# A two-layer decoder trunk on one core: the recurrent stage ordered by hand on four engines

## The chip, the core and the metric

The kernel runs on one core of a Trainium2 chip. A core has TensorE (matrix products, PE in the profile), VectorE (DVE), ScalarE (ACT), GpSimd (POOL), SyncE (SP, which here only issues DMAs), and DMA engines between the chip's memory and its own. The engines run side by side, each takes its own instructions strictly in order, and they wait for each other by semaphores. The metric is the device time of one execution in microseconds (us). Before the change it is 925.75 us, the median of three runs (925.34 to 928.98).

## What is computed

The input x is 1024 tokens by 1024 features, all float32. Two layers run one after the other; each has a projection, a token mixer, an attention over 256 fixed memory tokens, a SiLU gate, an output projection and a layer norm:

```python
for layer in range(2):
    if layer == 0:                      # multi-head latent attention, 12 heads
        z = h @ mla_w_in
        c_q, c_kv, k_r, gate, q_mem = split(z)
        q = rms_norm(c_q) @ w_uq;  kv = rms_norm(c_kv) @ w_ukv      # rotary part added
        tok = causal_attention(q, k, v)
    else:                               # recurrent branch, 768 channels
        z = h @ lru_w_in
        u, gate, q_mem = split(z)
        xc = conv_b + sum over 4 taps of shifted u * conv_w          # causal
        r = sigmoid(blockdiag(xc, w_r) + b_r);  i = sigmoid(blockdiag(xc, w_i) + b_i)
        log_a = (-8 * softplus(-lam)) * r;  a = exp(log_a)
        g = sqrt(-expm1(2 * log_a)) * (i * xc)
        tok[s] = a[s] * tok[s-1] + g[s]                              # scan over the tokens
    mem_out = softmax(q_mem @ mem_k.T / 8) @ mem_v                   # 4 heads, 256 tokens
    y = concat(tok, mem_out) * silu(gate)
    h = layer_norm(alpha * h + y @ w_out)
```

## The kernel before

Every float32 operand of a product is split into a rounded high part and the low rest, and one product is three matmuls: high by high, high by low, low by high (`mm3`, lines 110 to 115). The high part is a copy that rounds, made by ACT or POOL; the low part is a subtraction that only VectorE makes (`split`, lines 88 to 90). A weight tile comes by DMA into one of two stages `wf`, is split into a pair of buffers (a ring of two pairs, `R16`/`R17` and `rg0`/`rg1`), and is then used (`load_w`, line 100): the next load into a stage waits until both parts of the last have been made, and the next split into a pair waits until the products with the last are over.

The order on each engine comes from a scheduler that goes by the order of the code and by its own estimates, and may put later work first, except inside `manual_schedule`, where the engines named there keep the order of the code.

The stages, with their times in the profile: the compressed inputs and gates of layer 0 (to about 200 us), the causal attention (to about 440), the memory attention of layer 0 (to about 500), the output projection and layer norm of layer 0 (to about 593), the recurrent stage (593 to 710), the gate products (two of them to 733, the others between the units of the next stage), the memory attention of layer 1 (to about 807), the output projection of layer 1.

**Attention and the maxima rows.** Work is done in units of 512 columns: TensorE makes scores, ACT takes the exponential twice (full and rounded), and the low part is their difference (line 564), made by POOL, for every fourth unit by VectorE; TensorE then multiplies both parts with the values three units later. Between the units stands filler: the scores of the heads of the next pair, from which VectorE takes the row maxima (`max_pass`, lines 439 to 462). When a head's maxima are known, `neg_max_row` (line 427) puts a small job in a list: TensorE transposes the negated maxima (line 433), VectorE copies them (line 435), SP sends them by DMA into row 96 of that head's queries (line 436). The job is run `DELAY = 3` units later by `flush_rows`. The third score matmul of each tile of that head reads row 96 (97 rows, line 657).

**The products with the reciprocals.** When a pair of heads is done, `finish_pair` (line 624) sends the sums of the exponentials through memory and back as reciprocals, spread over the lanes, and POOL multiplies the pair's tile with them (line 634). The slots are 0 to 5 for the causal heads, 6 and 7 for the memory pairs of layer 0, 8 and 9 for those of layer 1. SP also loads layer norm's vectors into the same buffers `Of` afterwards.

**The recurrent stage** goes over six tiles t of 128 channels by 1024 tokens. `u`(t) is the projection on TensorE: 48 matmuls of 512 columns. `c`(t) copies it out of the PSUM banks (ACT, two halves, line 1015). `v`(t) is the convolution on VectorE (line 1020 and three times line 1023), then the high part XH (ACT, line 84) and the low part XL (VectorE, line 90). `r`(t) is all the rest (`lru_rest`): 12 gate matmuls of XH and XL with WGH and WGL, sigmoid (line 1036), exponential, tanh and square on ACT (lines 1038, 1039, 1041), three products and the scan on VectorE (lines 1040, 1042, 1044, 1045), a square root on ACT between them (line 1043). The code has `c0 v0 c1 v1 r0 u2 c2 v2 r1 u3 ...`, then the two projections of the memory queries (`q0`, `q1`) and two gate products (`g6`, `g7`). The weights of u0 and u1 come early into buffers of the attention; those of u2 to u5 are loaded in `lru_u`, and the gate weights WGH/WGL, both halves, before `c0`.

Of the kernel before, what the change touches and what calls it, by code (L numbers as in the profile page):

```python
# [20 lines left out]
S = 1024  # L21
# [23 lines left out]
def hybrid_kernel(ctx: ExitStack, tc: tile.TileContext, io):  # L45
# [209 lines left out]
    def qmem_proj(layer, m, ap, mh, ml, thi, tlo, ps):  # L255
        hi, lo = load_w(ap, S)
        proj_T(ps, hi, lo, mh, ml, 8)
        for n, cs in enumerate(HALF):
            ACT.copy(thi[n], ps[n])
            DVE.tensor_tensor(out=tlo[n], in0=ps[n], in1=f32(thi[n]), op=ALU.subtract)  # L260
            SP.dma_start(qmem_d[layer][m, 0][:, cs], f32(thi[n]))
            SP.dma_start(qmem_d[layer][m, 1][:, cs], f32(tlo[n]))

    for m in range(2):
        qmem_proj(0, m, io["w0"][8 + m], lambda n: [x[:, HALF[n]] for x in xh], lambda n: [x[:, HALF[n]] for x in xl],
                  ph[2 * m:2 * m + 2], pl[2 * m:2 * m + 2], next_ps())
# [160 lines left out]
    def neg_max_row(mx, dst_row):  # L427
# [9 lines left out]
        rows.append([DELAY, row])  # L437

    def max_pass(h, halves=None):
# [21 lines left out]
        neg_max_row(mx, lambda: sets[h % 4][2][96:97, :])  # L461
# [162 lines left out]
    def finish_pair(gt, slot):  # L624
# [9 lines left out]
        POOL.tensor_tensor(out=gt, in0=gt, in1=rec, op=ALU.mult)  # L634
# [325 lines left out]
    ring["hi"], ring["lo"] = [sets[i][2] for i in (1, 2, 3)], [sets[i][3] for i in (1, 2, 3)]  # L960
    u_ps = []
    for t in range(2):
        hi, lo = load_w(io["w1"][t], S)
        ps = pair(t)
        proj_T(ps, hi, lo, hth, htl, 8)
        u_ps.append(ps)
# [5 lines left out]
    ring["hi"], ring["lo"] = [R16, rg[0]], [R17, rg[1]]  # L972
    pc = open_pool("pc")
# [10 lines left out]
    for i in range(2):  # L984
        j = wjob[0]
        wjob[0] += 1
        SP.dma_start(wf[j % 2][:, 0:768], io["wg"][i])
        split(wf[j % 2][:, 0:768], WGH[:, i * 768:(i + 1) * 768], WGL[:, i * 768:(i + 1) * 768], POOL)

# [27 lines left out]
    def lru_conv(t):  # L1017
# [7 lines left out]
        split(xc, XH[b], XL[b], ACT)  # L1025

    def lru_rest(t):
# [52 lines left out]
    ORD = 'c0 v0 c1 v1 r0 u2 c2 v2 r1 u3 c3 v3 r2 u4 c4 v4 r3 u5 c5 v5 r4 q0 r5 q1 g6 g7'  # L1080
    for it in ORD.split():
        t = int(it[1])
        if it[0] == 'c':
            lru_copy(t, u_ps[t])
        elif it[0] == 'v':
            lru_conv(t)
        elif it[0] == 'r':
            lru_rest(t)
        elif it[0] == 'u':
            lru_u(t)  # L1090
        elif it[0] == 'g':
            gate_load(t)
            run_all(gate1(t, next_p()))
        else:
            qmem_proj(1, t, io["w1"][14 + t], hth, htl, [QH[:, c] for c in HALF], [QL[:, c] for c in HALF], next_p())
# [123 lines left out]
```

## Time and profile before

| | us |
|---|---|
| three runs, median (lowest to highest) | 925.75 (925.34 to 928.98) |
| the profiled execution, its own time | 924.84 |
| its span, first to last instruction | 923.0 |
| TensorE busy in the span | 896.5 (97%) |
| VectorE, ScalarE, GpSimd busy | 592.2 (64%), 443.1 (48%), 222.9 (24%) |
| mean granted TensorE clock, as a share of full speed | 0.992 |

The profile is one execution, 1.8 us longer outside its span than within it. A row of the timeline gives the start, the duration, the engine, the line and the operation with its tiles, and in brackets how long the engine had been idle before it and which instruction released it. Busy time of TensorE includes the overlap of pipelined matmuls, so that consecutive starts, not durations, give its pace. VectorE, ScalarE and GpSimd are far from full over the whole span, and nearly full in the recurrent stage.

### The profile page before, as it was taken

The page shows a single profiled execution, that of the slowest core. Times are in us where ns is not written, and L with a number is a line of the kernel's source. Part 1 is how long each engine was busy: PE and PEld are TensorE (multiplying, and loading weights), DVE is VectorE, ACT ScalarE, POOL GpSimd, SP SyncE. Part 2 cuts the span into 40 slices and gives each one's busy share as a digit, 9 for nine tenths or more (in the row PEclk, how much of TensorE's full clock was granted, in tenths as well). Part 3 has the DMA queues.
Part 4 walks back from the last instruction along what each step waited for, and adds up shares of the span by engine and source line. Part 5 has one row for each costly group of instructions (what it writes and reads, how often), then busy time and mean ns, then how long its engine had stood idle before and what let it go on. Part 6 is the DMA issues. An engine that isn't in the chain of part 4 may idle for free.

```text
span 923.0 us, 12452 instructions
## 1 busy us (share of the span) xinstructions
PE 896.5 (97%) x4477; PEld 735.2 (80%) x4477; DVE 592.2 (64%) x1207; ACT 443.1 (48%) x764; POOL 222.9 (24%) x219
## 2 busy tenths in 40 slices
PE   9999999999999999999999999988999999999996
PEld 8998888877787788778777888867888877678886
DVE  7953346258867767796775497646997154457655
ACT  4422311217676667777795122107997156753000
POOL 5100023101526364563672200000000032210000
PEclk9999999999999999999999999998999999999998
DMA  9103133314022213056657653111113921252411
GB/s 328 45 15 109 55 100 127 128 63 111 23 61 70 59 58 104 13 144 178 194 150 207 197 194 125 50 51 47 45 46 113 220 69 47 69 184 91 155 73 46
DMA packets 45945, 96.08 MB, mean 104 GB/s; under 512 B 10906, under 2 KB 20282, under 8 KB 45884
## 3 DMA queue, kind: packets, MB, share of 16 engines
q1 hardware_dynamic: 45308, 94.47, 32.7%
q8 instruction: 35, 0.57, 0.3%
q10 hardware_dynamic: 576, 0.82, 0.3%
q14 instruction: 26, 0.21, 0.1%
HBM read 71.94 MB, written 23.16 MB: 103 GB/s over the span
## 4 chain that ended last, share of the span: by engine, by line
PE 82%; DVE 7%; ACT 3%; issue 3%; DMA 2%; POOL 2%; SPq 0%; DVEq 0%; ACTq 0%; POOLq 0%
PE bank L113 10%; PE bank L115 10%; PE bank L114 10%; PE bank L858 6%; PE bank L860 6%; PE bank L859 6%; PE bank L572 6%; PE bank L657 5%; PE bank L367 3%; PE bank L369 3%; PE bank L368 3%; PE bank L154 2%; PE bank L155 2%; PE bank L153 2%; PE bank L454 2%
## 5 line engine op out<-in xcount | busy, mean ns | idle before, releaser
L564 POOL TENSOR_TENSOR pl<-Pf,ph 128x512 fp32r<-128x512 f32 (+1 forms) x99 | 124.6, 1268 | 116.4 <-ACT ph L562 93.6
L561 ACT ACTIVATE Pf<-bank 128x512 f32<-128x512 f32 (+1 forms) x152 | 86.3, 568 | 50.3 <-DVE bank L558 20.8
L657 PE MATMUL bank<-st,st 96*128 96x512 f32 (+7 forms) x432 | 105.5, 342 | 0.1
L90 DVE TENSOR_TENSOR R<-wf,R 128x1024 fp32r<-128x1024 f32 (+4 forms) x43 | 48.8, 1138 | 65.6 <-POOL R L82 59.8
L657 PEld LDWEIGHTS bank<-st,st 96*128 96x128 f32 (+1 forms) x432 | 75.7, 189 | 13.0 <-DVE st L403 0.5
L562 ACT ACTIVATE ph<-bank 128x512 fp32r<-128x512 f32 (+1 forms) x136 | 76.2, 561 | 0.2
L82 POOL TENSOR_SCALAR R<-wf 128x1024 fp32r<-128x1024 f32 (+3 forms) x25 | 24.4, 979 | 200.1 <-PE bank L114 97.3
L113 PE MATMUL bank<-R,R 128*128 128x256 f32 (+1 forms) x190 | 63.2, 333 | 0.7 <-ACT Pf L375 0.4
L114 PE MATMUL bank<-R,R 128*128 128x256 f32 (+1 forms) x190 | 62.3, 328 | 0.1
L115 PE MATMUL bank<-R,R 128*128 128x256 f32 (+1 forms) x190 | 62.2, 327 | 0.0
L456 DVE CUSTOM_DVE_ANT_0 bank<-bank,cmask 128x384 f32<-128x384 f32 (+3 forms) x96 | 48.8, 517 | 9.8 <-PE bank L454 9.0
L123 ACT ACTIVATE rq_t<-lnv 128x1 f32<-128x1 f32 x16 | 3.3, 203 | 101.7 <-DVE lnv L909 101.7
L367 PE MATMUL bank<-xh,R 128*128 128x512 f32 x128 | 50.8, 397 | 0.1
L369 PE MATMUL bank<-xh,R 128*128 128x512 f32 x128 | 50.7, 396 | 0.0
L368 PE MATMUL bank<-xl,R 128*128 128x512 f32 x128 | 50.5, 395 | 0.0
L572 PE MATMUL bank<-ph,VH 128*65 128x512 f32 (+2 forms) x144 | 49.2, 342 | 0.0
L572 PE MATMUL bank<-pl,VH 128*65 128x512 f32 (+2 forms) x144 | 44.8, 338 | 2.2 <-POOL pl L564 1.2
L572 PE MATMUL bank<-ph,VL 128*65 128x512 f32 (+2 forms) x144 | 47.0, 337 | 0.0
L859 PE MATMUL bank<-wo,yh 128*128 128x512 f32 (+1 forms) x126 | 46.8, 371 | 0.0
L858 PE MATMUL bank<-wo,yh 128*128 128x512 f32 (+1 forms) x126 | 46.6, 369 | 0.0
L860 PE MATMUL bank<-wo,yl 128*128 128x512 f32 (+1 forms) x126 | 46.0, 369 | 0.0
L904 DVE SCALAR_TENSOR_TENSOR GA<-GA,bank 128x512 f32<-128x512 f32 (+1 forms) x34 | 22.0, 647 | 37.1 <-PE bank L860 37.1
(315 smaller groups left out, 2447.1 us busy)
## 6 DMA issues: line engine op xcount, KB each, us to landing
wf<-w SPq DMA_DIRECT2D x26, 512.0 KB
wf<-wout SPq DMA_DIRECT2D x16, 512.0 KB
Of<-den_d SPq DMA_DIRECT2D x20, 256.0 KB
GA<-x SPq DMA_DIRECT2D x8, 512.0 KB
h_d<-GA SPq DMA_DIRECT2D x8, 512.0 KB
GA<-h_d SPq DMA_DIRECT2D x8, 512.0 KB
y_d<-GA SPq DMA_DIRECT2D x7, 512.0 KB
out<-GA SPq DMA_DIRECT2D x7, 512.0 KB
```

The lines of the kernel that those rows point to most:

```text
L113: PE.matmul(out, lh, rh, start=(i == 0), stop=False)
L114: PE.matmul(out, lh, rl, start=False, stop=False)
L115: PE.matmul(out, ll, rh, start=False, stop=(i == n - 1))
L367: PE.matmul(ps[n], hi[:, ks], xh[k][:, cs], start=(k == 0), stop=False)
L369: PE.matmul(ps[n], lo[:, ks], xh[k][:, cs], start=False, stop=(k == 7))
L561: ACT.activation(pf[:, :n], ps[:, :n], AF.Exp, scale=scale)
L564: lo_eng.tensor_tensor(out=lo[:, :n], in0=pf[:, :n], in1=f32(hi)[:, :n], op=ALU.subtract)
L572: mm.append(lambda: PE.matmul(ops[0:65, q0:q0 + w], st, mv[:, c0:c0 + w], start=start, stop=stop))
L657: yield lambda: PE.matmul(ps[:, c0:c0 + w], k[0:r, ks], q[0:r, qs], start=(i == 0), stop=(i == 2))
L858: PE.matmul(out, hi, woh[k][:, ns], start=(k == ko[0]), stop=False)
L859: PE.matmul(out, hi, wol[k][:, ns], start=False, stop=False)
L860: PE.matmul(out, lo, woh[k][:, ns], start=False, stop=(k == ko[7]))
```

## The change

1. The recurrent stage is cut into finer pieces, and their order is written out for VectorE, ScalarE, GpSimd and TensorE at once (`manual_schedule`): `x` is the low part XL, `s` the gate matmuls and sigmoids, `i` the product of input gate and convolution, `e` exponential, tanh and square, `n` the product under the root, `z` root, product and scan, `w` the second half of the gate weights, `l`, `k`, `h` loads and splits of weights ahead of their use.
2. XH is copied by GpSimd, not ScalarE.
3. The weights of u2 and u3 are loaded and split before u0's products, the first half of the gate weights after them, the second half between tiles 0 and 1. u1's weights go into another free pair of attention buffers.
4. The products with the reciprocals of slots 7, 8 and 9 are made by VectorE, not GpSimd.
5. The maxima row of an even head is run 5 units after its maxima, not 3.

```diff
-    def neg_max_row(mx, dst_row):
+    def neg_max_row(mx, dst_row, delay=DELAY):
...
-        rows.append([DELAY, row])
+        rows.append([delay, row])
...
-        neg_max_row(mx, lambda: sets[h % 4][2][96:97, :])
+        neg_max_row(mx, lambda: sets[h % 4][2][96:97, :], 5 if h % 2 == 0 else DELAY)
...
-        POOL.tensor_tensor(out=gt, in0=gt, in1=rec, op=ALU.mult)
+        eng = DVE if slot >= 7 else POOL
+        eng.tensor_tensor(out=gt, in0=gt, in1=rec, op=ALU.mult)
...
-    ring["hi"], ring["lo"] = [sets[i][2] for i in (1, 2, 3)], [sets[i][3] for i in (1, 2, 3)]
+    ring["hi"], ring["lo"] = [sets[i][2] for i in (1, 3)], [sets[i][3] for i in (1, 3)]
     u_ps = []
+    uw = [load_w(io["w1"][t], S) for t in range(2)]
+    ring["hi"], ring["lo"] = [R16], [R17]
+    gw = {2: load_w(io["w1"][2], S)}
     for t in range(2):
-        hi, lo = load_w(io["w1"][t], S)
+        hi, lo = uw[t]
...
     ring["hi"], ring["lo"] = [R16, rg[0]], [R17, rg[1]]
+    gw[3] = load_w(io["w1"][3], S)
...
-    for i in range(2):
+
+    def lru_wg(i):
...
-        split(xc, XH[b], XL[b], ACT)
-
-    def lru_rest(t):
+        hi_copy(POOL, XH[b], xc)
+
+    def lru_gates(t):
...
-        a = G1[t]
-        ACT.activation(a, rr, AF.Exp, scale=cf[:, t:t + 1])
-        ACT.activation(rr, rr, AF.Tanh, scale=cf[:, t:t + 1])
-        DVE.tensor_tensor(out=ii, in0=ii, in1=xc, op=ALU.mult)
-        ACT.activation(xc, a, AF.Square)
-        DVE.scalar_tensor_tensor(out=rr, in0=xc, scalar=1.0, in1=rr, op0=ALU.add, op1=ALU.mult)
-        ACT.activation(rr, rr, AF.Sqrt, scale=-1.0)
-        DVE.tensor_tensor(out=ii, in0=rr, in1=ii, op=ALU.mult)
-        DVE.tensor_tensor_scan(out=G1[t], data0=a, data1=ii, initial=0.0, op0=ALU.mult, op1=ALU.add)
+
+    def lru_low(t):
+        b = t % 2
+        DVE.tensor_tensor(out=XL[b], in0=XC[b], in1=f32(XH[b]), op=ALU.subtract)
+
+    def lru_in(t):
+        b = t % 2
+        DVE.tensor_tensor(out=II[b], in0=II[b], in1=XC[b], op=ALU.mult)
+
+    def lru_decay(t):
+        b = t % 2
+        ACT.activation(G1[t], RR[b], AF.Exp, scale=cf[:, t:t + 1])
+        ACT.activation(RR[b], RR[b], AF.Tanh, scale=cf[:, t:t + 1])
+        ACT.activation(XC[b], G1[t], AF.Square)
+
+    def lru_norm(t):
+        b = t % 2
+        DVE.scalar_tensor_tensor(out=RR[b], in0=XC[b], scalar=1.0, in1=RR[b], op0=ALU.add, op1=ALU.mult)
+
+    def lru_scan(t):
+        b = t % 2
+        ACT.activation(RR[b], RR[b], AF.Sqrt, scale=-1.0)
+        DVE.tensor_tensor(out=II[b], in0=RR[b], in1=II[b], op=ALU.mult)
+        DVE.tensor_tensor_scan(out=G1[t], data0=G1[t], data1=II[b], initial=0.0, op0=ALU.mult, op1=ALU.add)
...
-    ORD = 'c0 v0 c1 v1 r0 u2 c2 v2 r1 u3 c3 v3 r2 u4 c4 v4 r3 u5 c5 v5 r4 q0 r5 q1 g6 g7'
+    ORD = ('c0 v0 c1 x0 s0 u2 v1 i0 e0 x1 n0 w1 z0 '
+           'c2 s1 u3 v2 i1 e1 x2 n1 l4 z1 '
+           'c3 s2 u4 v3 i2 e2 x3 n2 l5 z2 '
+           'c4 s3 u5 v4 i3 e3 x4 n3 k0 z3 '
+           'c5 s4 v5 i4 e4 x5 n4 k1 z4 q0 '
+           's5 i5 e5 n5 h6 z5 q1 h7 g6 g7')
+    with tc.manual_schedule(engines={E.DVE, E.Activation, E.Pool, E.PE}):
+        for it in ORD.split():
...
```

What the change moves on VectorE at the start of the recurrent stage. The rows are its instructions in order; U0 and U1 are the copied projections of tiles 0 and 1, XC, XH, XL the convolution and its parts, R17 and rg1 low parts of later weights. Before:

```order
L1020 TENSOR_SCALAR XC0_5392<-U0_5390,vecs_69 128x1024
L1020 TENSOR_SCALAR XC1_5393<-U1_5391,vecs_69 128x1024
L1023 SCALAR_TENSOR_TENSOR XC0_5392<-U0_5390,vecs_69,XC0_5392 128x1024
L1023 SCALAR_TENSOR_TENSOR XC1_5393<-U1_5391,vecs_69,XC1_5393 128x1024
L1023 SCALAR_TENSOR_TENSOR XC0_5392<-U0_5390,vecs_69,XC0_5392 128x1024
L1023 SCALAR_TENSOR_TENSOR XC1_5393<-U1_5391,vecs_69,XC1_5393 128x1024
L1023 SCALAR_TENSOR_TENSOR XC0_5392<-U0_5390,vecs_69,XC0_5392 128x1024
L1023 SCALAR_TENSOR_TENSOR XC1_5393<-U1_5391,vecs_69,XC1_5393 128x1024
L90 TENSOR_TENSOR XL0_5396<-XC0_5392,XH0_5394 128x1024
L90 TENSOR_TENSOR R17_71<-wf0_82,R16_70 128x1024
L90 TENSOR_TENSOR XL1_5397<-XC1_5393,XH1_5395 128x1024
```

and with the change, the same place on VectorE:

```order
L1028 TENSOR_SCALAR XC0_5398<-U0_5396,vecs_69 128x1024
L1031 SCALAR_TENSOR_TENSOR XC0_5398<-U0_5396,vecs_69,XC0_5398 128x1024 x3
L1048 TENSOR_TENSOR XL0_5402<-XC0_5398,XH0_5400 128x1024
L1028 TENSOR_SCALAR XC1_5399<-U1_5397,vecs_69 128x1024
L1031 SCALAR_TENSOR_TENSOR XC1_5399<-U1_5397,vecs_69,XC1_5399 128x1024 x3
L1052 TENSOR_TENSOR II0_5406<-II0_5406,XC0_5398 128x1024
L1048 TENSOR_TENSOR XL1_5403<-XC1_5399,XH1_5401 128x1024
L1062 SCALAR_TENSOR_TENSOR RR0_5404<-XC0_5398,RR0_5404 128x1024
L90 TENSOR_TENSOR WGL_5411<-wf1_83,WGH_5410 128x768
L1067 TENSOR_TENSOR II0_5406<-RR0_5404,II0_5406 128x1024
L1068 SCALAR_TENSOR_TENSOR GA0_72<-GA0_72,II0_5406 128x1024
```

Tile 0's convolution and low part stood interleaved with tile 1's, whose first instruction needs U1; now tile 0 is finished first.

What it moves on TensorE behind the last matmul of u1 (its first row below). Before:

```order
L115 MATMUL bank3_87<-HTh1_4566,st2_3_1787 128x512
L113 MATMUL bank4_88<-HTh0_4565,R16_70 128x512
L114 MATMUL bank4_88<-HTl0_4567,R16_70 128x512
L113 MATMUL bank5_89<-HTh1_4566,R16_70 128x512
L114 MATMUL bank5_89<-HTl1_4568,R16_70 128x512
L113 MATMUL bank2_86<-HTh0_4565,rg0_5385 128x512
L114 MATMUL bank2_86<-HTl0_4567,rg0_5385 128x512
L113 MATMUL bank3_87<-HTh1_4566,rg0_5385 128x512
L114 MATMUL bank3_87<-HTl1_4568,rg0_5385 128x512
L113 MATMUL bank6_90<-XH0_5394,WGH_5404 128x512
L113 MATMUL bank7_91<-XH0_5394,WGH_5404 128x512
L113 MATMUL bank0_84<-XH0_5394,WGH_5404 128x512
```

and with the change:

```order
L115 MATMUL bank3_87<-HTh1_4566,st3_3_1791 128x512
L113 MATMUL bank6_90<-XH0_5400,WGH_5410 128x512
L114 MATMUL bank6_90<-XL0_5402,WGH_5410 128x512
L115 MATMUL bank6_90<-XH0_5400,WGL_5411 128x512
L113 MATMUL bank7_91<-XH0_5400,WGH_5410 128x512
L114 MATMUL bank7_91<-XL0_5402,WGH_5410 128x512
L115 MATMUL bank7_91<-XH0_5400,WGL_5411 128x512
```

Eight matmuls of u2 and u3 that needed only high parts of their weights stood ahead of tile 0's gate matmuls; now the 12 gate matmuls follow u1 at once, and the 48 of u2 follow them.

What it moves on VectorE near the end of layer 1's memory attention; mpl1 to mpl3 are low parts of the exponentials, GB2 and GB3 the tiles of its two pairs, Of0 the reciprocals. Before:

```order
L564 TENSOR_TENSOR mpl1_6089<-Pf1_77,mph1_6085 128x512
L564 TENSOR_TENSOR mpl2_6090<-Pf2_78,mph2_6086 128x512
L621 TENSOR_TENSOR GB3_5384<-bank3_87,GB3_5384 64x512
L564 TENSOR_TENSOR mpl3_6091<-Pf3_79,mph3_6087 128x512
L621 TENSOR_TENSOR GB3_5384<-bank4_88,GB3_5384 64x512
```

and with the change:

```order
L564 TENSOR_TENSOR mpl1_6092<-Pf1_77,mph1_6088 128x512
L635 TENSOR_TENSOR GB2_5386<-GB2_5386,Of0_80 128x1024
L564 TENSOR_TENSOR mpl2_6093<-Pf2_78,mph2_6089 128x512
L621 TENSOR_TENSOR GB3_5387<-bank3_87,GB3_5387 64x512
L564 TENSOR_TENSOR mpl3_6094<-Pf3_79,mph3_6090 128x512
L621 TENSOR_TENSOR GB3_5387<-bank4_88,GB3_5387 64x512
```

The product of slot 8, which stood on GpSimd, now stands between two low parts.

## Rows read from the trace of the kernel before

**Rows 1.** The page: busy time of each engine.

```profile
PE 896.5 (97%) x4477; PEld 735.2 (80%) x4477; DVE 592.2 (64%) x1207; ACT 443.1 (48%) x764; POOL 222.9 (24%) x219
```

**Rows 2.** TensorE's waits: waiter, releaser, us in total, times, longest.

```profile
PE bank L113 <- ACT XH L84: 6.9, 1, 6.9
...
PE bank L572 <- DVE mpl L564: 1.2, 1, 1.2
...
PE bank L433 <- DVE mx L456: 0.9, 2, 0.5
```

**Rows 3.** Timeline of TensorE in the recurrent stage: start, us, what [idle, releaser].

```profile
616.56 0.39 PE L113 MATMUL bank<-HTh,R 128*128 128x512 f32 x1
...
625.43 2.08 PE L113 MATMUL bank<-XH,WGH 128*128 128x512 f32 x4 [6.86 <-ACT XH L84]
...
630.72 0.63 PE L115 MATMUL bank<-HTh,R 128*128 128x512 f32 x1
...
670.96 0.39 PE L113 MATMUL bank<-HTh,rg 128*128 128x512 f32 x1
...
710.13 0.39 PE L113 MATMUL bank<-HTh,R 128*128 128x512 f32 x1
```

**Rows 4.** Timeline of VectorE at the start of the recurrent stage.

```profile
607.47 1.51 DVE L1020 TENSOR_SCALAR XC<-U,vecs 128x1024 f32<-128x1024 f32 x1 [4.87 <-POOL R L82]
617.45 0.81 DVE L1020 TENSOR_SCALAR XC<-U,vecs 128x1024 f32<-128x1024 f32 x1 [8.48 <-ACT U L1015]
618.18 7.26 DVE L1023 SCALAR_TENSOR_TENSOR XC<-U,vecs,XC 128x1024 f32<-128x1024 f32 x6
```

**Rows 5.** Timeline of ScalarE: the same place, and one later step.

```profile
624.33 2.19 ACT L84 CAST XH<-XC 128x1024 fp32r<-128x1024 f32 x2 [6.99 <-DVE XC L1023]
...
655.05 1.28 ACT L1036 ACT_TABLE_LOAD   x1
...
662.34 1.04 ACT L1041 ACTIVATE XC<-GA 128x1024 f32<-128x1024 f32 x1
```

**Rows 6.** Stretches: length, busy us of five engines (instructions), clock, DMA share, GB/s.

```profile
625.40:631.10 5.70, 5.67 (x13) 4.46 (x14) 4.64 (x5) 4.56 (x6) 0.00 (x0) 0.50 0.28 96
657.00:671.00 14.00, 14.00 (x62) 11.30 (x61) 12.85 (x12) 12.54 (x16) 1.05 (x1) 1.00 0.12 39
```

**Rows 7.** Lines 1044 and 1045: duration ns min/median/max; a GpSimd copy.

```profile
L1044 DVE TENSOR_TENSOR II<-RR,II x6: 1226/1240/2007, 639.3 to 709.0; 128x1024 f32<-128x1024 f32 x6
L1045 DVE TENSOR_TENSOR_SCAN GA<-GA,II x4: 2280/2282/2291, 642.8 to 684.4; 128x1024 f32<-128x1024 f32 x4
654.27 1.05 POOL L82 TENSOR_SCALAR rg<-wf 128x1024 fp32r<-128x1024 f32 x1 [11.98 <-PE bank L114]
```

**Rows 8.** Timeline at the end of layer 0's last norm.

```profile
596.87 1.28 DVE L914 SCALAR_TENSOR_TENSOR GA<-GA,rq_y,Of 128x1024 f32<-128x1024 f32 x1
598.32 1.03 PE L931 MATMUL bank<-ident,GA 128*128 128x128 f32 x8
```

**Rows 9.** Timeline near the end of layer 1's memory attention, three engines.

```profile
799.67 2.39 POOL L634 TENSOR_TENSOR GB<-GB,Of 128x1024 f32<-128x1024 f32 x1 [6.86 <-DMA Of<-den_d]
800.55 2.65 DVE L564 TENSOR_TENSOR mpl<-Pf,mph 128x512 fp32r<-128x512 f32 x2 [1.79 <-ACT mph L562]
803.95 0.69 DVE L564 TENSOR_TENSOR mpl<-Pf,mph 128x512 fp32r<-128x512 f32 x1
802.65 0.45 PE L572 MATMUL bank<-mpl,VH 128*65 128x512 f32 x1 [1.25 <-DVE mpl L564]
```

**Rows 10.** Timeline at a maxima row of head 4; a small DMA and its reader.

```profile
289.44 0.27 PE L433 MATMUL bank<-ident,nm 128*8 128x128 f32 x1 [0.47 <-DVE mx L456]
297.83 0.87 PE L657 MATMUL bank<-st,st 96*128 96x512 f32 x3
790.35 0.54 SPq L627 DMA_DIRECT2D rn<-den  x1
793.28 0.24 DVE L628 RECIPROCAL rn<-rn 128x16 f32<-128x16 f32 x1
```

More of the change, by code (lines that the diff above doesn't have):

```diff
@@ L253, in hybrid_kernel, with qmem_proj @@
     HALF = [slice(0, 512), slice(512, 1024)]
-    def qmem_proj(layer, m, ap, mh, ml, thi, tlo, ps):
-        hi, lo = load_w(ap, S)
+    def qmem_proj(layer, m, w, mh, ml, thi, tlo, ps):
+        hi, lo = w
         proj_T(ps, hi, lo, mh, ml, 8)
@@ L264, in hybrid_kernel @@
     for m in range(2):
-        qmem_proj(0, m, io["w0"][8 + m], lambda n: [x[:, HALF[n]] for x in xh], lambda n: [x[:, HALF[n]] for x in xl],
+        qmem_proj(0, m, load_w(io["w0"][8 + m], S), lambda n: [x[:, HALF[n]] for x in xh], lambda n: [x[:, HALF[n]] for x in xl],
                   ph[2 * m:2 * m + 2], pl[2 * m:2 * m + 2], next_ps())
@@ L988, in hybrid_kernel @@
         split(wf[j % 2][:, 0:768], WGH[:, i * 768:(i + 1) * 768], WGL[:, i * 768:(i + 1) * 768], POOL)
+    lru_wg(0)
     CW, CB, BR, BI, LAM = 5, 29, 35, 41, 47
@@ L1053, in lru_u @@
     def lru_u(t):
-        hi, lo = load_w(io["w1"][t], S)
+        hi, lo = gw.pop(t)
         ps = next_p()
@@ L1057, in lru_u @@
         u_ps.append(ps)
-    gw = {}
     gorder = [6, 7, 0, 1, 2, 3, 4, 5]
@@ L1078, in gate1 @@
             yield
-    ORD = 'c0 v0 c1 v1 r0 u2 c2 v2 r1 u3 c3 v3 r2 u4 c4 v4 r3 u5 c5 v5 r4 q0 r5 q1 g6 g7'
[L1081 to L1095, printed above, removed]
+    ORD = ('c0 v0 c1 x0 s0 u2 v1 i0 e0 x1 n0 w1 z0 '
[5 rows of a table added]
+    E = mybir.EngineType
+    with tc.manual_schedule(engines={E.DVE, E.Activation, E.Pool, E.PE}):
+        for it in ORD.split():
+            t = int(it[1])
+            ops = {'c': lambda t: lru_copy(t, u_ps[t]), 'v': lru_conv, 'x': lru_low, 's': lru_gates, 'i': lru_in,
+                   'e': lru_decay, 'n': lru_norm, 'z': lru_scan, 'w': lru_wg, 'u': lru_u, 'h': gate_load,
+                   'g': lambda t: run_all(gate1(t, next_p()))}
+            if it[0] in ops:
+                ops[it[0]](t)
+            elif it[0] == 'l':
+                gw[t] = load_w(io["w1"][t], S)
+            elif it[0] == 'k':
+                gw[t + 20] = load_w(io["w1"][14 + t], S)
+            else:
+                qmem_proj(1, t, gw.pop(t + 20), hth, htl, [QH[:, c] for c in HALF], [QL[:, c] for c in HALF], next_p())
     close_pool(pc)
```

## The prediction, made before the changed kernel was run

> **What bounds the kernel now.** I read the page's busy line first: TensorE works 896.5 of 923.0 us, 97% [rows 1], so only what lets it wait less, or run at a higher clock, can move the end. Then the list of its waits [rows 2]. One stands out: 6.9 us, once, at the first gate matmul of the recurrent stage, ended by ScalarE's XH. The others that the change touches are 1.2 us (a low part in a memory unit) and 0.9 us (two maxima rows). The timelines of the stage then say why XH0 is late. VectorE begins tile 0's convolution at 607.47, but its second instruction is tile 1's and waits 8.48 us, until 617.45, for U1, which needs u1, just finished on TensorE [rows 4]. So tile 0's three taps end only at 625.44 beside tile 1's, and XH0 starts at 624.33 [rows 5]. TensorE, which issued its first u2 matmul at 616.56, gets through the eight that need high parts alone, and stands 6.86 us [rows 3]. The stall costs a second time. In the stretch right behind it the granted clock is 0.50, the lower level, 1.2 GHz, against 1.00 later [rows 6].
>
> **The recurrent stage, the main term.** I price it from both ends instead of adding up stalls. Between the first u2 matmul (616.56) and the first gate product g6 (710.13) lie 93.57 us [rows 3]. They hold 360 matmuls of 512 columns: six projections of 48 and six gate sets of 12. Undisturbed, from 670.96 to 710.13, 168 of them (u5, q0, q1 and two gate sets) take 39.17 us, so 0.2332 us each [rows 3]. At that pace the 360 take 83.95, and 9.62 us are lost. The parts agree: 6.86 of waiting, and 625.43 to 630.72 for 12 matmuls that take 2.80 at pace, so 2.49 of low clock, together 9.35. The change does the same 360 matmuls, gate set first. If nothing waits, 9.6 us go.
>
> Does s0 start without a wait? In TensorE's new order u0's last matmul stands five places later, 5 x 0.2332 = 1.17 us, so the first XC0 instruction starts near 608.6 instead of 607.47. Four convolution instructions take about 1.51 plus three of 7.26 / 6 = 1.21 [rows 4]: end at 613.8. A GpSimd copy of this size takes 1.05 [rows 7], so XH0 is there near 614.8 and XL0, if like the product of the same size 1.24 [rows 7], near 616.1. TensorE ends u1 near 616.6, since the sum of its work ahead is the same. The margin is 1.7 us for XH0 and, since XL0 is wanted only a matmul later, 0.7 for XL0. If c0 came 1 us later, s0 would wait about 0.3.
>
> Then each step of 60 matmuls lasts 60 x 0.2332 = 13.99 us, and the four engines have to fit into it. Call T the start of a gate set. U(t+1) is there at about T + 0.9 (617.45 against 616.56 for U1 now [rows 3, 4]) and its convolution done at T + 5.8. The product i (1.24) and XL (1.24) follow, to T + 8.3; each can lie beside a GpSimd copy, and L1044 grew from 1.226 to 2.007, by 0.78, beside the one at 654.27 [rows 7], so at most T + 9.8. TensorE asks for XH and XL only at T + 14: over 4 us spare, which is what hides the added copies. VectorE's sum per step is 12.85 of 14.00 now [rows 6]; one more GpSimd copy beside it makes 13.63, still less. ScalarE falls from 12.54 by XH's 1.10 (half of 2.19 [rows 5]) to 11.4. The tight one is the serial chain of one tile: sigmoid to square takes ScalarE from the table load at 655.05 to 663.38, 8.33 us [rows 5], so the square is done near T + 8.9. Then n (1.24), a weight's low part (1.24), the root on ScalarE beside it, the product (1.24) and the scan (2.28 [rows 7]) make T + 14.9, and the next convolution could begin at T + 14.9 instead of 13.99 + 0.9 + T. They are level; a drift of 0.4 a step, 2 us over five, stays within the 4 us spare. So I take the full 9.6, bounds 7.0 and 9.6.
>
> GpSimd and VectorE beside each other are the point in the design that could speak against it: six new copies, and a row in which VectorE's product grew by 0.78 next to one [rows 7]. By the rows six copies cost VectorE up to 4.7 us. The Trainium skill, page SBUF — State Buffer, section Who interferes with whom, is harsher: a VectorE instruction with two inputs in SBUF and a GpSimd instruction that reads there exclude each other, and whoever comes second is blocked for the whole instruction. By that rule the six cost up to 6 x 1.05 = 6.3 us, an estimate; the row shows three quarters of it, and by neither does TensorE wait while 4 us are spare.
>
> **Weights and the norm of layer 0.** The loads of u2's and u3's weights take the early places that the gate weights had, and their splits stand before u0. One of these low parts, 1.2 us on VectorE, now stands before the norm's last instruction at 596.87. TensorE has four or five of u1's matmuls (about 1.1 us) to do ahead of the last transposes at 598.32 [rows 8]. Bounds 0 and -1.2; I take -0.2. SP's issues only change which weight comes first; behind a load that waits on a stage stand stores that nothing awaits within this stage.
>
> **The products with the reciprocals.** In slot 8 GpSimd's 2.39 us product lies beside two low parts of VectorE, which take 2.65 for the two where a later one takes 0.69, and TensorE waits 1.25 us for the first, until 802.65 [rows 9]. With the change mpl1 starts at 800.55 and is done at 801.24, the product follows (1.24, to 802.5), and mpl2 ends near 803.2. TensorE, 1.25 us earlier than now, asks for mpl1 at 801.4 and for mpl2 some seven matmuls later, near 803.0. Gain 1.0; bounds -0.2 (the product delays mpl2 by more than I take) and 1.25. By the skill's rule just named mpl1 would be blocked to 802.06 and done 0.69 later, at 802.75; TensorE went on at 802.65, so the trace agrees here. In slots 7 and 9 no wait of TensorE hangs on the product: 0, bounds -0.5 (VectorE waits for `Of`) and 0.5.
>
> **The maxima rows.** Two of them, each waiting on VectorE, cost 0.9 [rows 2]; the even heads' rows move 14 to 19 places later in TensorE's order, so the maxima are there by then. The price is that the row lands later. For head 4: 289.44 + 18 places of at most 0.233 gives 293.6 at worst; transposes 0.27, a copy behind at most one VectorE instruction (about 1.5 with it), a small DMA 2.9 (790.35 to the reader at 793.28), so 298.3. The row is read by the third matmul of the group at 297.83, that is at 298.4 [rows 10]. Just in time. Gain up to 0.9, loss of some 0.5 in each of three heads if the DMA is slower; bounds -1.5 and 0.9, I take 0.4.
>
> **The sum.** 9.6 - 0.2 + 1.0 + 0.4 = 10.8. The profiled execution took 924.84, so 914.0; the median of the runs is 0.9 above it: 914.9, rounded to 914.8. Bounds together: 9.6 + 0 + 1.25 + 0.5 + 0.9 = 12.3 at best (913.5), 7.0 - 1.2 - 0.2 - 0.5 - 1.5 = 3.6 at worst (922.2).
>
> **Rivals.**
> (a) The later maxima rows come too late. For: the margin above is 0.1 us by its worst figures. Against: the 18 places hold shorter matmuls too. -1.5 instead of 0.4: 916.7.
> (b) s0 still waits. If VectorE, ahead of c0, is held by the early splits or the gate weight, XL0 comes 1 to 2 us late; TensorE has nothing else ahead in its fixed order, and after a stall of that kind the clock stood at 0.50 for 12 matmuls, 2.5 us [rows 3, 6]. 1.5 + 2.5 = 4.0 back: 918.8.
> (c) Slower: the written-out order ties VectorE, ScalarE and GpSimd to a chain per step that is longer than TensorE's step, since scan, product and root of one tile stand before the next convolution. If nothing overlaps, it is 0.9 + 8.33 + 1.24 + 1.24 + 1.04 (the root, as the square [rows 5]) + 1.24 + 2.28 + 2 x 0.78 = 17.8 us against 13.99. Five steps of 3.8, less 4 to 5 us of cushion, lose 14 to 15, more than the 10.8 won: about 929.4. It turns the sign from an excess of (10.8 + 5) / 5 = 3.2 us a step, a chain of 17.2. Against: the root runs beside the low part, and copies by GpSimd seldom lie beside both products.
> (d) The stall moves, to s1 or s2 say, and nothing is won but the small terms: 924.
>
> **How the numbers follow.** Forecast 0.66, (a) 0.14, (b) 0.10, (d) 0.06, (c) 0.04. What a measurement can tell is 0.5%, 4.6 us, so 921.1 is the line for faster: forecast, (a) and (b) lie below it, 0.90; (d) is no change, 0.06; (c) slower, 0.04. The range runs from 911.5, 2 us beyond the best sum since the pace itself may gain in the stretches where the clock was low, to 919.5, which takes in (a) and (b); outside lie (c), (d) and a little of the rest.
>
> **What would show it.** Right: no wait for XH in TensorE's list, granted clock 1.00 from 616 to 640, first g6 matmul near 700.5, 14.0 us from u to u, VectorE under 14 busy in a step. Slot 8: the wait for mpl at most 0.3. Rows: no wait for the maxima of even heads, and no new wait of line 657 on a DMA. Wrong: a wait of TensorE for XL or XH in s1 to s5, which grows from step to step, is (c); one at s0 alone, with a clock of 0.5 behind it, is (b); the same g6 start near 710 with the waits elsewhere is (d).

## The result and the profile after

| | before | after |
|---|---|---|
| first comparison, four runs each, median (lowest to highest), us | 927.17 (925.34 to 928.98) | 914.47 (912.29 to 916.22) |
| second comparison, 11 and 5 runs | 926.71 (924.36 to 930.84) | 914.75 (913.26 to 915.95) |
| profiled execution / its span | 924.84 / 923.0 | 916.22 / 914.4 |

The ratio is 0.9862 with a 95% interval of 0.9826 to 0.9898, and 0.9866 (0.9840 to 0.9892) in the second comparison. The forecast was 914.8.

The page's busy line, to be read beside [rows 1]: the same 4477 matmuls, in a span that is 8.6 us shorter (923.0 and 914.4).

```profile
PE 894.0 (98%) x4477; PEld 733.0 (80%) x4477; DVE 599.5 (66%) x1210; ACT 437.1 (48%) x758; POOL 227.5 (25%) x222
```

TensorE's waits after (waiter, releaser, us in total, times, longest). None of the three lines of [rows 2] is left: XH, mpl and the rows' L433 are gone. But the second line here is new.

```profile
PE bank L572 <- POOL pl L564: 2.4, 3, 1.3
PE bank L861 <- DVE R L838: 1.9, 1, 1.9
```

**The recurrent stage.** TensorE's timeline at the last matmul of u1, the start of the first gate set and the first g6 matmul, to be read against [rows 3]:

```profile
619.39 0.39 PE L115 MATMUL bank<-HTh,st 128*128 128x512 f32 x1
619.62 0.39 PE L113 MATMUL bank<-XH,WGH 128*128 128x512 f32 x1
619.85 0.40 PE L114 MATMUL bank<-XL,WGH 128*128 128x512 f32 x1
...
703.44 0.39 PE L113 MATMUL bank<-HTh,R 128*128 128x512 f32 x1
```

The gate set follows u1 without a gap, and the 360 matmuls from 619.62 to 703.44 take 83.82 us where they took 93.57: 9.75 less, or 0.2328 us each, the undisturbed pace. The windows (length, busy us of TensorE, its weight loads, VectorE, ScalarE, GpSimd, then clock, DMA share, GB/s) show the clock at 1.00 from the start of the stage, where [rows 6] had 0.50; the second is one later step:

```profile
616.00:640.00 24.00, 24.00 (x105) 19.40 (x104) 19.79 (x17) 17.83 (x21) 4.01 (x4) 1.00 0.08 23
645.00:659.00 14.00, 14.00 (x62) 11.31 (x61) 12.92 (x10) 11.59 (x13) 2.88 (x2) 1.00 0.12 37
```

VectorE's timeline of the first steps, and two copies of GpSimd beside it:

```profile
612.54 3.93 DVE L1031 SCALAR_TENSOR_TENSOR XC<-U,vecs,XC 128x1024 f32<-128x1024 f32 x3
617.63 1.23 DVE L1048 TENSOR_TENSOR XL<-XC,XH 128x1024 fp32r<-128x1024 f32 x1 [1.17 <-POOL XH L82]
620.44 0.81 DVE L1028 TENSOR_SCALAR XC<-U,vecs 128x1024 f32<-128x1024 f32 x1 [1.58 <-ACT U L1023]
...
634.87 0.79 DVE L1028 TENSOR_SCALAR XC<-U,vecs 128x1024 f32<-128x1024 f32 x1
...
639.54 1.22 DVE L1052 TENSOR_TENSOR II<-II,XC 128x1024 f32<-128x1024 f32 x1
641.70 2.06 DVE L1048 TENSOR_TENSOR XL<-XC,XH 128x1024 fp32r<-128x1024 f32 x1 [0.94 <-POOL XH L82]
...
649.49 0.79 DVE L1028 TENSOR_SCALAR XC<-U,vecs 128x1024 f32<-128x1024 f32 x1
...
685.55 2.05 DVE L1048 TENSOR_TENSOR XL<-XC,XH 128x1024 fp32r<-128x1024 f32 x1 [0.95 <-POOL XH L82]
```

```profile
639.80 1.86 POOL L82 TENSOR_SCALAR XH<-XC 128x1024 fp32r<-128x1024 f32 x1 [11.73 <-DVE XC L1031]
641.63 1.05 POOL L82 TENSOR_SCALAR R<-wf 128x1024 fp32r<-128x1024 f32 x1
```

Three things are to be read here. XL0 ends at 618.86 and is wanted at 619.85, 1.0 us to spare. The convolutions start 14.43 and then 14.62 us apart, against TensorE's 13.99: VectorE is now the slower of the two, by 0.6 a step. XL of tile 1 had 4.7 us to spare (done at 629.13, wanted at 633.81). And this spare time shrinks: XL of tile 5 ends at 687.60, and TensorE asks for it at 689.69. Six tiles end before it is used up.

**Slot 8.** VectorE's timeline, and the matmul that had waited 1.25 us [rows 9]:

```profile
793.42 0.69 DVE L564 TENSOR_TENSOR mpl<-Pf,mph 128x512 fp32r<-128x512 f32 x1 [1.79 <-ACT mph L562]
794.03 1.22 DVE L635 TENSOR_TENSOR GB<-GB,Of 128x1024 f32<-128x1024 f32 x1
795.17 0.68 DVE L564 TENSOR_TENSOR mpl<-Pf,mph 128x512 fp32r<-128x512 f32 x1
```

```profile
794.17 0.44 PE L572 MATMUL bank<-mpl,VH 128*65 128x512 f32 x1
```

The product is 1.22 us between two low parts of 0.69, and nothing waits.

**The new wait lies outside the change.** Slot 6 still has its product on GpSimd. After the change, TensorE, VectorE and GpSimd at 496 us, and the clock of the stretch:

```profile
496.11 2.44 POOL L635 TENSOR_TENSOR GA<-GA,Of 128x1024 f32<-128x1024 f32 x1 [3.33 <-DMA Of<-den_d]
496.24 3.46 DVE L838 TENSOR_TENSOR R<-R,R 128x512 fp32r<-128x512 f32 x2
499.16 0.50 PE L861 MATMUL bank<-VH,R 128*128 128x512 f32 x1 [1.86 <-DVE R L838]
```

```profile
500.00:505.00 5.00, 5.00 (x16) 3.91 (x15) 1.36 (x3) 1.20 (x2) 0.00 (x0) 0.66 0.56 177
```

and before, the same two instructions:

```profile
498.39 2.42 POOL L634 TENSOR_TENSOR GA<-GA,Of 128x1024 f32<-128x1024 f32 x1 [4.67 <-DMA Of<-den_d]
...
497.18 1.28 DVE L837 TENSOR_TENSOR R<-R,R 128x512 fp32r<-128x512 f32 x2
```

The product starts when a DMA lands: 498.39 before, when VectorE was just finishing the two low parts; 496.11 in this execution, just ahead of them, and they take 3.46 us instead of 1.28. TensorE waits 1.86 us, and the clock drops behind it. So the profiled executions differ like this, by the starts of the same matmul in both: 0.94 won up to 496 (0.56 of it in the first 15 us, which the change doesn't touch; see the last section), 3.66 lost at slot 6, 0.34 lost at the norm of layer 0, 9.75 won in the recurrent stage, 0.43 in the gate products (no run takes this apart), 1.50 from slot 8 on: 8.62 in all. Without slot 6 it would be 12.3, which is near the 12.7 and 12.0 of the medians.

### The profile page after: what moved, and what is told of

It is laid out like the page before. It is cut to its first block, busy times and chain, and to the rows that moved or that the text cites. A ratio compares the mean times of both kernels' runs of the same rounds, so it can differ in the third digit from the quotient of the medians.

```text
span 914.4 us, 12466 instructions
## 1 busy us (share of the span) xinstructions
PE 894.0 (98%) x4477; PEld 733.0 (80%) x4477; DVE 599.5 (66%) x1210; ACT 437.1 (48%) x758; POOL 227.5 (25%) x222
## 4 chain that ended last, share of the span: by engine, by line
PE 87%; DVE 6%; ACT 2%; DMA 2%; issue 2%; POOL 1%; SPq 0%; DVEq 0%; ACTq 0%; POOLq 0%
PE bank L113 10%; PE bank L114 10%; PE bank L115 10%; PE bank L572 8%; PE bank L860 7%; PE bank L861 7%; PE bank L859 7%; PE bank L658 6%; PE bank L367 3%; PE bank L369 3%; PE bank L368 3%; PE bank L454 2%; PE bank L154 2%; PE bank L155 2%; PE bank L153 2%; DVE st L403 2%
```

## The experiments

The main theory (A): the recurrent order is worth 9.6 or so by itself, because VectorE finishes tile 0 first; the products and rows add a little over 1 us; slot 6 is an accident of timing. The rivals are named with each run. "Changed kernel with slot 6" is e1 of experiment 5, and the base of several others. Part 3, the earlier loads of weights, was not put back by itself.

**1. The parts apart.** `e3_recurrent_only` puts back parts 4 and 5:

```diff
-        eng = DVE if slot >= 7 else POOL
+        eng = POOL
-        neg_max_row(mx, lambda: sets[h % 4][2][96:97, :], 5 if h % 2 == 0 else DELAY)
+        neg_max_row(mx, lambda: sets[h % 4][2][96:97, :], DELAY)
```

> The changed recurrent stage alone: products of slots 7 to 9 on GpSimd and the maxima rows after 3 units, as before. Theory A: the stage gives 9.8 us less 0.3 for the norm, so 9.5 below the kernel before in a like run (about 915.5 against 925; with the collision at slot 6 both 3.6 higher); TensorE's 1.25 us wait for mpl and the 0.9 us at the maxima rows are there again. Rival: parts 4 and 5 are worth more than 2 us, since GpSimd's products slow VectorE elsewhere too; then it is at 917 or above without the collision.

`e4_products_rows_only` puts parts 4 and 5 alone into the kernel before:

```diff
-        POOL.tensor_tensor(out=gt, in0=gt, in1=rec, op=ALU.mult)
+        (DVE if slot >= 7 else POOL).tensor_tensor(out=gt, in0=gt, in1=rec, op=ALU.mult)
-        neg_max_row(mx, lambda: sets[h % 4][2][96:97, :])
+        neg_max_row(mx, lambda: sets[h % 4][2][96:97, :], 5 if h % 2 == 0 else DELAY)
```

> The kernel before with products of slots 7 to 9 on VectorE and the later maxima rows only; the recurrent stage is as before. Theory A: 1.25 us at slot 8 and 0.4 us at the rows, so about 1.7 below before in a like run (923.3; with the collision at slot 6 927), and the 6.9 us wait for XH with the clock at 0.50 behind it is unchanged. Rival: 3 us or more below before, or nothing because VectorE's waits for the reciprocals cost what GpSimd's slowing did.

Measured: e3 916.81, ratio 0.9900 (0.9881 to 0.9919), with kernel before at 925.49, so 8.7 less by the medians; e4 923.78, ratio 0.9982 (0.9968 to 0.9996), 1.7 less. Together 10.4, the whole change 12.0 to 12.7; the intervals allow both. In e3 the stage is 83.82 us long, as in the changed kernel, and its trace has the waits of parts 4 and 5 again; in e4 the wait for XH stands as it was:

```profile
794.68 0.45 PE L572 MATMUL bank<-mpl,VH 128*65 128x512 f32 x1 [1.25 <-DVE mpl L564]
```

```profile
627.01 2.08 PE L113 MATMUL bank<-XH,WGH 128*128 128x512 f32 x4 [6.84 <-ACT XH L84]
```

```profile
627.00:632.00 5.00, 4.99 (x12) 3.95 (x13) 4.62 (x5) 4.03 (x5) 0.00 (x0) 0.52 0.28 88
```

Within the noise the parts add up, as theory A has it. e3's rival, parts 4 and 5 worth more than 2 us, would need 917 without the accident at slot 6; e3's profiled execution (916.85) has the accident, a wait of 1.89 us (below), and 915.0 without it, where theory A has 915.5. Whether its other four runs had the accident no trace shows, and the times alone (e3 lies 2.1 above the changed kernel's 914.75, taken on another chip) don't exclude the rival. The traces do not bear it out: from slot 8 to the end e4 wins 1.50 us on the kernel before, as the changed kernel does, and the rows give about 0.5 (experiment 4).

**2. One place in VectorE's order put back.** Tile 1's convolution ahead of tile 0's low part; base: the changed kernel with slot 6.

```diff
-    ORD = ('c0 v0 c1 x0 s0 u2 v1 i0 e0 x1 n0 w1 z0 '
+    ORD = ('c0 v0 c1 v1 x0 s0 u2 i0 e0 x1 n0 w1 z0 '
```

> The changed kernel with the slot 6 product on VectorE, and in the written order tile 1's convolution ahead of tile 0's low part (c0 v0 c1 v1 x0 s0 ...): only that one place in VectorE's order is put back. Theory A (the order on VectorE at the start of the stage is the whole main term): XL0 comes only about 6.8 us after the end of u1, TensorE waits about 6.6 us at the first XL matmul, the clock falls to the lower level behind it, 2 to 2.5 us more; about 9 us slower than the same kernel without it (922 to 923). Rival B: XH by GpSimd and the early gate weights carry part of the gain, then it loses 5 us or less. Rival C: the clock stays up, then 6.6 us (920).

Measured: 921.87, 4.0 below its kernel before (925.83; ratio 0.9966, 0.9945 to 0.9987), where the base was 12.1 below. The stage from the first gate matmul to g6 takes 92.01 us (617.01 to 709.02). Its timeline:

```profile
617.01 0.40 PE L113 MATMUL bank<-XH,WGH 128*128 128x512 f32 x1
623.86 0.79 PE L114 MATMUL bank<-XL,WGH 128*128 128x512 f32 x1 [6.46 <-DVE XL L1048]
...
627.31 0.40 PE L113 MATMUL bank<-XH,WGH 128*128 128x512 f32 x1
```

One low part that stands behind U1 in VectorE's order brings back 8.2 of the 9.75 us: 6.46 of waiting, the rest the lower clock of the matmuls behind it, 0.43 us apart until 627. From 623.86 to 627.31 eight matmuls took 3.45 us instead of 1.87; the low clock ended before the gate set did, which is why it is 8.2 and not 9. Rival B (5 us or less) and C (the clock stays up) fall.

**3. XH by ScalarE in the new order**, base as in 2.

```diff
-        hi_copy(POOL, XH[b], xc)
+        hi_copy(ACT, XH[b], xc)
```

> The changed kernel with the slot 6 product on VectorE and XH copied by ScalarE in the same written order (between the sigmoids and the exponential of the tile before). Theory A: ScalarE then waits for the convolution before it goes on, the square comes 2.1 us later in each step, VectorE's step grows from 14.6 to about 16.6 us, the spare time of XL (5 us at tile 1) is used up near tile 4, and TensorE waits about 2.5 us each at tiles 4 and 5, with a lower clock behind: 5 to 9 us slower (918 to 922). Rival B: ScalarE's sum per step (11.4 + 1.1) stays below 14 us and nothing waits: 913 to 914. So part 2 of the change is needed only if A holds.

Measured: 921.67 (ratio 0.9954, 0.9935 to 0.9972); the stage takes 92.59 us. Four rows of VectorE's timeline, one of ScalarE's, and one of the three waits of TensorE:

```profile
650.91 0.79 DVE L1028 TENSOR_SCALAR XC<-U,vecs 128x1024 f32<-128x1024 f32 x1
...
661.37 1.23 DVE L1062 SCALAR_TENSOR_TENSOR RR<-XC,RR 128x1024 f32<-128x1024 f32 x1 [3.37 <-ACT XC L1058]
662.52 1.22 DVE L90 TENSOR_TENSOR rg<-wf,rg 128x1024 fp32r<-128x1024 f32 x1
...
667.21 0.79 DVE L1028 TENSOR_SCALAR XC<-U,vecs 128x1024 f32<-128x1024 f32 x1
```

```profile
655.69 1.05 ACT L84 CAST XH<-XC 128x1024 fp32r<-128x1024 f32 x1 [3.59 <-DVE XC L1031]
```

```profile
663.79 0.51 PE L115 MATMUL bank<-HTh,rg 128*128 128x512 f32 x1 [2.12 <-DVE rg L90]
```

ScalarE waits 3.59 us for the convolution in front of XH, the square comes late, VectorE's n waits 3.37 us for it, and the step grows to 16.30 us. The size is theory A's (expected step 16.6), the place is not: TensorE waited three times, 2.1 us each, not for XL but for the low part of the weights of u5, q0 and q1, which stands behind n on VectorE. In the changed kernel that low part (the weights' `rg`) ends at 660.63 and is used at 664.73, so it has 4 us. Rival B, by busy sums alone, falls: ScalarE's 12.5 us would have fitted into 14. Tile 0's gate set runs without a wait here too (XH's first matmul at 616.23, XL's at 616.46), so the engine that makes XH is not what stalled the stage before.

**4. The rows, later and earlier.** e7 runs even heads' rows after 7 units, e11 after 3 as before; base as in 2.

```diff
-        neg_max_row(mx, lambda: sets[h % 4][2][96:97, :], 5 if h % 2 == 0 else DELAY)
+        neg_max_row(mx, lambda: sets[h % 4][2][96:97, :], 7 if h % 2 == 0 else DELAY)
```

> The changed kernel with the slot 6 product on VectorE and the maxima rows of even heads run 7 units after the maxima, not 5. Theory A (the prediction's working: at 5 units the row lands within 0.1 us of its need by the worst figures, so two units more are too late): TensorE waits for the DMA of the row at the third score matmul in three to five heads, 1.5 to 3 us each, 5 to 12 us slower. Rival B: the working was too strict and there were some us to spare; then 0 to 2 us slower.

```diff
-        neg_max_row(mx, lambda: sets[h % 4][2][96:97, :], 5 if h % 2 == 0 else DELAY)
+        neg_max_row(mx, lambda: sets[h % 4][2][96:97, :], DELAY)
```

> The changed kernel with the slot 6 product on VectorE and the maxima rows of even heads run after 3 units as before: part 5 undone. Theory A: the two waits of 0.45 us at the rows are there again and the wait for the row maxima near 315 us stays: 0.4 to 0.9 us slower than the same kernel with part 5. Rival: another 1 us or more, or nothing, since low parts wait there anyway.

Measured: e7 915.28 and 919.58 (two runs). Its trace has no wait for a row in any head. One new wait, 1.56 us, ends with an exponential of ScalarE, which had stood behind a weight cast that waited for its load:

```profile
421.01 0.73 PE L658 MATMUL bank<-st,st 96*128 96x512 f32 x2 [1.56 <-ACT ph L562]
```

```profile
418.80 1.05 ACT L84 CAST R<-wf 128x1024 fp32r<-128x1024 f32 x1 [2.48 <-DMA wf<-wmk]
419.87 0.60 ACT L561 ACTIVATE Pf<-bank 128x512 f32<-128x512 f32 x1
```

This wait came of the edit, but not of a late row: in e1 the same exponential starts at 418.03, ahead of the cast at 419.35; with the rows at 7 units the scheduler put the cast first. It moved matmuls too. The third score matmul of head 4's first tile, which reads the row, follows the other two at once in the changed kernel; in e7 seventeen others stand between, the first twelve of them filler. The changed kernel, then e7:

```profile
297.08 0.87 PE L658 MATMUL bank<-st,st 96*128 96x512 f32 x3
```

```profile
297.04 0.63 PE L658 MATMUL bank<-st,st 96*128 96x512 f32 x2
297.50 0.39 PE L113 MATMUL bank<-R,R 128*128 128x512 f32 x1
...
300.93 0.99 PE L658 MATMUL bank<-st,st 96*128 96x384 f32 x5
```

By the semaphore updates in the traces head 4's row has landed at 295.95 in the changed kernel and is read at 297.56, 1.6 us to spare; in e7 it has landed at 298.61, 1.1 us behind the old place of its reader in the order (near 297.5), and is read at 301.29. So e7 does not show that a row after 7 units lands in time for the order that the changed kernel has.

e11: 915.65 (ratio 0.9873, 0.9847 to 0.9899) beside 913.69 for its base on the same chip (0.9857, 0.9832 to 0.9883). Its list of waits has the rows' line back, as [rows 2] has it:

```profile
PE bank L433 <- DVE mx L456: 0.9, 2, 0.5
```

But the starts of the same matmuls on both sides of such a wait show that only half of it is won. From before to behind head 4's row, and again head 8's, a kernel with the later rows gains 0.23 to 0.26 us on one without, in each of five pairs of profiles (the changed kernel against before and e3, e4 against before, e1 and e10 against e11). The rest is lost at the next wait for VectorE's row maxima, here in the changed kernel, where the matmul starts 0.48 us after the one before it instead of 0.23 (PEld is TensorE's weight load):

```profile
293.54 0.40 PE L572 MATMUL bank<-ph,VL 128*65 128x512 f32 x1
294.02 0.19 PEld L454 LDWEIGHTS bank<-st,st 96*128 96x128 f32 x1 [0.57 <-DVE mx L456]
294.02 0.50 PE L454 MATMUL bank<-st,st 96*128 96x512 f32 x1
```

So five units win about 0.5 us, not the 0.9 of the list of waits. The 2.0 us between the medians of e11 and its base are more than that, and their intervals overlap.

**5. Slot 6.** e1 (and e10, again) is the changed kernel with

```diff
-        eng = DVE if slot >= 7 else POOL
+        eng = DVE if slot >= 6 else POOL
```

> The changed kernel with the slot 6 product on VectorE too. Theory A: in the profile of the changed kernel TensorE lost about 3.65 us at 498 to 503 (1.86 us waiting for a low part of line 838, then a lower clock), because GpSimd's slot 6 product landed beside it; whether it lands there is decided by when a DMA arrives, so some runs have it (916) and some not (912.5). Then here every run is at 912 to 913, with a spread under 1.5 us, and the two L838 together take about 1.3 us instead of 3.46. Rival B: the loss has another cause in the changed kernel; then runs near 916 stay. Rival C: VectorE now waits for the same DMA in front of the last L838; then TensorE gets a new wait of 1 to 2 us there and the time is 914 to 917 in every run.

e2 is the kernel before with that one product moved:

```diff
-        POOL.tensor_tensor(out=gt, in0=gt, in1=rec, op=ALU.mult)
+        (DVE if slot == 6 else POOL).tensor_tensor(out=gt, in0=gt, in1=rec, op=ALU.mult)
```

> The kernel before with only the slot 6 product on VectorE; TensorE's order is unchanged. Theory A: the same collision makes the spread of the kernel before (925.3 to 929.0), so here all runs are at 925 to 926, spread under 1.5 us. Rival B: the collision belongs to the change alone and the spread of before comes from elsewhere; then runs near 925 and near 929 both stay.

e9 is the changed kernel once more, on the chip of e10.

> The changed kernel itself, timed again beside the next two. Theory A: its four first runs (912.3 to 916.2) are spread by waits of 1 to 2 us that a lower clock follows in some runs and not in others; median 913 to 915, spread 3 us or more, 10.5 to 12.7 below the kernel before. Rival: the median lies above 915.5, and the first comparison was a lucky one.

> The changed kernel with the slot 6 product on VectorE, again, on the same chip as the changed kernel. Theory A: the wait of 1.9 us at 499 us is gone in every run, and with it the lower clock behind it where that came: 1 to 2.5 us below the changed kernel. Rival: another wait of about the same size takes its place (as where all products went to VectorE), within 0.7 us of the changed kernel.

Measured: e1 913.44 (913.02 to 914.85), e10 913.69 (912.97 to 914.61), e9 914.75 (913.26 to 915.95); e2 926.52 (924.10 to 930.02) beside 925.49. In e1 the low parts take 1.29 us for the two, as theory A has it, and the product follows them, without a wait of TensorE:

```profile
498.59 1.29 DVE L838 TENSOR_TENSOR R<-R,R 128x512 fp32r<-128x512 f32 x2
...
500.62 1.23 DVE L635 TENSOR_TENSOR GA<-GA,Of 128x1024 f32<-128x1024 f32 x1
```

The collision is chance: the changed kernel had it in its first profile and not in the second, where the product came at 499.31; e3 had it too, the kernel before and e4 had not. That half of theory A holds. The other half, that slot 6 makes the spread of runs, fell: e2 spreads over 5.9 us, as the kernel before does (7.5 beside it), and e1 over 1.8, with a run at 914.85, where all were to lie at 912 to 913. What e1 and e10 win on the changed kernel, some 1.1 us by the medians (the ratios 0.9857 and 0.9866 have overlapping intervals), is not resolved as a gain; it is the fastest version here by its medians. Where else the spread comes from is in part this: behind a wait of this size the clock falls in one execution and not in another. e3's wait at the same place was as long as the changed kernel's, and its clock stayed at 1.00:

```profile
499.84 0.50 PE L861 MATMUL bank<-VH,R 128*128 128x512 f32 x1 [1.89 <-DVE R L838]
```

```profile
500.00:505.00 5.00, 5.00 (x22) 4.03 (x23) 2.01 (x4) 1.20 (x2) 0.00 (x0) 1.00 0.57 192
```

**6. All ten products on VectorE.** `eng = DVE`, in the changed kernel.

> The changed kernel with the products of all ten slots on VectorE. TensorE's waits that are left at 410, 447 and 484 us (1.33, 1.13, 0.76 us in the changed kernel) each stand 3 to 6 us behind a 2.4 us product on GpSimd, which delays the low parts that GpSimd makes. Theory A: these three go, 2 to 3 us, and the lower clock that some runs show behind such a wait goes too: 910 to 911.5 with less spread. Rival B: VectorE, which takes its work in order, waits for the reciprocals' DMA in front of row maxima and low parts, and TensorE gets other waits of the same size: 913 to 915.

Measured: 914.48 (ratio 0.9883, 0.9867 to 0.9899), and not 910 to 911.5: rival B. VectorE takes its work in order and waits for the reciprocals itself:

```profile
444.54 2.05 DVE L635 TENSOR_TENSOR GA<-GA,Of 128x1024 f32<-128x1024 f32 x1 [1.32 <-DMA Of<-den_d]
```

TensorE's three waits behind GpSimd's products shrink, and others (0.8 at 408 us for row maxima, 0.7 at 448 for an exponential) take their place.

## Why the prediction was right, and where it was off

**The main term** was 9.6 and measured 9.75. Experiment 1 shows that parts 1 to 3 alone give it (83.82 us in e3), and experiment 2 that the named cause carries it: one low part behind tile 1's convolution brings the wait and the low clock back, 8.2 us. That experiment 3 loses 8.8 by another change says that the two are not shares of one sum: the order must be right at the start and in every step. To price the stage from both ends, instead of from the wait of 6.86, gave the clock's part without knowing how it works. The margin at s0 came out as worked out: 1.0 us for XL0 against 0.7. One reading in the working is loose: 625.44 is the end of all six taps, tile 1's too; XH0 starts at 624.33 because tile 0's taps had ended by then.

**VectorE's step.** The prediction let it drift by 0.4 us a step inside 4 us of cover; it drifts by 0.62, and the cover fell from 4.7 at tile 1 to 2.1 at tile 5. And the tight chain is another. The prediction took the one through ScalarE's square; but the square ends at 642.70, and n starts only at 643.68, without a wait for it, because VectorE is still at XL:

```profile
641.65 1.05 ACT L1058 ACTIVATE XC<-GA 128x1024 f32<-128x1024 f32 x1
```

```profile
643.68 1.21 DVE L1062 SCALAR_TENSOR_TENSOR RR<-XC,RR 128x1024 f32<-128x1024 f32 x1
```

So VectorE's own row of instructions sets the step, with its wait for XH in it. The copies on GpSimd cost a little more than the 0.78 each from [rows 7]: XH at 639.80 takes 1.86 where it takes 1.05 alone, because the product i began 0.26 us ahead of it, so VectorE starts XL at 641.70 instead of 640.85; then XL takes 2.06 beside the next copy. That is 0.85 + 0.83 = 1.7 us a step on VectorE. The rule of the Trainium skill (SBUF — State Buffer, Who interferes with whom) fits these rows better than the 0.78 did: i ends at 640.76, and 1.05 behind that is 641.81, measured 641.66; the next copy ends at 642.68, and XL's 1.23 behind that is 643.91, measured 643.76. It also fits slot 6: GpSimd ends at 498.55, two low parts of 0.64 make 499.83, measured 499.70. None of it reached TensorE in the recurrent stage, as forecast.

**Rival (c)**, a chain longer than TensorE's step, did not decide, but it was the right thing to fear: experiment 3 makes the step 16.30 us by moving one copy, and 8.8 us of the stage go.

**Slot 8** was taken at 1.0: mpl2 was ready at 795.85 and asked for at 796.08, so the whole 1.25 came, and the profile shows 1.50 from there to the end. **The norm** cost 0.34, taken as 0.2.

**The rows** were taken at 0.4 out of a possible 0.9, for fear of a late row. About 0.5 came, but for another reason (half of each wait comes back at the next one), so this term is right by luck. The row of head 4, which the working takes, was not near being late: the margin was worked out as 0.1 us and is 1.6. The working took 2.9 us for a small DMA, from its issue at 790.35 to a reciprocal at 793.28 [rows 10]. But the reciprocal stood behind a low part in VectorE's order, and did not start when the DMA landed:

```profile
792.45 0.91 DVE L564 TENSOR_TENSOR mpl<-Pf,mph 128x512 fp32r<-128x512 f32 x1 [4.29 <-ACT mph L562]
```

By the semaphore updates that DMA had landed at 792.36, 2.0 us behind its issue; head 4's row in the changed kernel takes 1.8 (294.13 to 295.95).

**What the sum left out** is slot 6. The prediction read slots 7 to 9 and took the part of the program between them as it stood in one profile. There a product on GpSimd, whose start hangs on a DMA, began just as two low parts ended (498.39 and 498.46); a DMA that lands 2 us earlier makes that a loss of 3.66 us. By the sum the profiled time should have been 914.0; it was 916.22, and 12.3 less than before without this; the first g6 matmul, forecast near 700.5, started at 703.44.

**Luck.** The forecast of 914.8 and the median of 914.47 lie closer than the sum deserves. The kernel before had a median of 927.17 in that comparison, 1.4 us above the 925.75 that the sum started from. And in the profiled execution the 3.66 us of slot 6, which the sum left out, stand against 1.5 that it left out as well: 0.56 in the first 15 us, 0.43 in the gate products and 0.5 from slot 8 on.

## What to carry to other kernels

When an engine that works in order stands in the middle of two tiles' work, look at which instruction of the later tile stands ahead of the earlier one's last: here one instruction that waited for U1 cost nearly 10 us of a stage, and its place, not the engine that makes XH, was the cause. Price a stage with a stall by its count of matmuls at the undisturbed pace: that holds the clock's part as well. And when a busy sum fits into the step, follow the chain in order of issue as well: in experiment 3, XH on an engine with time to spare made the step 2 us too long. A wait that disappears from the list is not yet time won: look at the next wait for the same engine.

## What the runs showed of the hardware that was not expected

Whether a lower clock follows a wait of TensorE varied from one execution to the next. Of ten waits of 1.5 to 2.2 us in these profiles six were followed by it (1.86 us in the changed kernel; 1.69, 1.68 and 1.66 near 449 us in e1, e9 and e11; 1.56 in e7; 2.14 at 696 us in e6), four were not (1.89 in e3; 1.56 at slot 8 in e2; 2.12 and 2.06 in e6). The four waits of 6.46 to 6.86 us all were. The wait of 1.30 us near 230 us stands in every profile here and was followed by the lower clock once, in e4, with 0.75 for the stretch from 230 to 235. In the changed kernel the drop cost 1.63 us on top of the wait at 499 (the loss against before grows from 2.03 at the first matmul behind it to 3.66).

The first 15 us vary too, between executions of one program. In the stretch from 5.6 to 9.2 us five of the thirteen profiles have 17 or 18 matmuls and eight 12 or 13: the changed kernel has 18, the kernel before 13, e10 has 18, and e1, the same program, 12. That is where the 0.56 us come from that the changed kernel is ahead before the change begins; no run shows what decides it.
